# The last store of a row-sum kernel, split by partitions over two issuing engines

## The chip, the cores and the metric

The kernel runs on one core of a Trainium2 chip. The metric is the device time of one execution in microseconds (us); lower is better. Three runs of the kernel before took 160.67, 160.80 and 160.85 us, so its time is their median, 160.8 us.

A core has several engines that run side by side and wait for each other through semaphores. Three matter here: VectorE (DVE in the profile) and ScalarE (ACT) do the arithmetic; SyncE (SP) computes nothing and issues DMAs, the transfers between HBM and the on-chip memory SBUF. ScalarE can issue DMAs too. SBUF has 128 partitions; a transfer of a tile moves one row for each partition.

## The reference

```
batch, seq, dim = 32, 512, 1024
x: (32, 512, 1024) float32, multiplier: 0.5

return (np.sum(x, axis=-1) * multiplier).astype(np.float32)
```

The input has 32 x 512 = 16384 rows of 1024 floats, 64 MB in all. Each row gives one number, so the output is 64 KB.

## The kernel before

Each of the 128 partitions takes 128 rows, in 8 blocks of 16. In the first 7 blocks (112 rows of each partition, `own = 112`) the rows of a partition lie one behind the other in the input; the last block is cut the same way from what is left (`x_last`, `out_last`). So a block is a tile of 128 partitions x 16 rows x 1024 floats, 8 MB, and there are three buffers for blocks (`buf`). The sums of the rows are collected in the tile `res`, 128 partitions x 128 columns, of which the last 16 columns belong to the last block.

SyncE issues all transfers, in the order in which they stand in the code. The loads of the first three blocks are moved ahead of the program's opening barrier (`start_loads_at_entry`); each later load (line 76, the helper `load`) waits until VectorE has done with the block that was in its buffer. The last block comes in five pieces: three into a block's buffer (10 rows, 4 rows, one row and 384 columns of the last), and the rest of the last row into the small tile `end`.

Blocks 0 to 5 are summed on VectorE with one reduction each (line 121) and scaled by the multiplier into `res` (line 127). Of block 6, VectorE sums 8 rows and ScalarE the other 8, one activation per row with an accumulated sum (line 85). Then SyncE issues the early store of the first 112 columns of `res` (line 169). The 16 rows of the last block are shared out: rows 1, 4, 7, 9, 13 and 14 to ScalarE, the others to VectorE (line 95, the helper `dve_sum`). The last row is summed in three cuts by VectorE, and its third sum, `final`, takes the first two in.

The end of the program is what the change touches. `late_act` is the count of the semaphore `act_done` after ScalarE's last row; `done` is the count of `dve_done` after `final`. SyncE waits for `act_done` (line 194), then issues the last store, of the last 16 columns of `res` in all 128 partitions (8 KB, 64 bytes per partition), which itself waits for `dve_done` (line 195). Then it waits until the early store and this one have landed (lines 199 and 200, one instruction in the program). The engines end their programs there, and a closing stretch follows that is not part of the span.

Of the kernel before, what the change touches and what calls it, by code (L numbers as in the profile page):

```python
# [9 lines left out]
def kernel(  # L10
# [13 lines left out]
    nc = tc.nc  # L24
# [4 lines left out]
    P = nc.NUM_PARTITIONS  # L29
# [12 lines left out]
    own = rows - B  # L42
# [3 lines left out]
    out_last = out_flat[P * own : N].rearrange("(p c) -> p c", p=P)  # L46

    def sbuf(name, *shape):
        return ctx.enter_context(nc.sbuf_tensor(name, list(shape), fp32)).ap()
# [4 lines left out]
    res = sbuf("res", P, rows)  # L54
# [4 lines left out]
    def sem(name):  # L59
        return nc.alloc_semaphore(name=name)  # L60

    dve_done = sem("dve_done")
    act_done = sem("act_done")
    counts = {"dve": 0, "act": 0}

    def marks(i, engine):

        s = dve_done if engine == "dve" else act_done
        i.then_inc(s, 1)
        counts[engine] += 1  # L70
        return counts[engine]
# [36 lines left out]
    for b in range(n_blocks - 1):  # L108
# [11 lines left out]
        done = marks(  # L120
            nc.vector.reduce_sum(  # L121
                out=sums[:, c0 : c0 + h], in_=t[:, 0:h, :], axis=mybir.AxisListType.X
            ),
            "dve",
        )
        freed.append(done)
        scaled = nc.vector.tensor_single_scalar(  # L127
            out=res[:, c0 : c0 + h],
            in_=sums[:, c0 : c0 + h],
# [45 lines left out]
    for k, (lo, hi) in enumerate(((0, 10), (10, 14), (14, 15))):  # L175
# [4 lines left out]
        late_act = marks(i, "act") if k == len(landed) - 1 else None  # L180
# [10 lines left out]
    final.wait_op(landed_end[1], 17, "sem-ge")  # L191
    done = marks(final, "dve")

    nc.sync.wait_ge(act_done, late_act)
    store = nc.sync.dma_start(out=out_last, in_=res[:, own:])
    store.wait_op(dve_done, done, "sem-ge")
    stored = sem("stored")
    store.then_inc(stored, 16)
    nc.sync.wait_ge(early_stored, 16)
    nc.sync.wait_ge(stored, 16)  # L200

    def start_loads_at_entry(nc_):

# [60 lines left out]
```

## Time and profile before

| | |
|---|---|
| median of three runs | 160.8 us |
| span of the profiled execution, first to last instruction of the program | 159.3 us |
| loads of x | 67.11 MB, DMA engines busy 98.1% of the span |
| VectorE busy | 119.8 us (75%) |
| ScalarE busy | 16.3 us (10%) |
| last store, issue on SyncE | 157.89 us, 0.34 us long |
| last store, issue to landing | 1.4 us |
| waits at the end (line 200) | 28 ns from 159.3 us |

The profile is of one execution, and its times count from the first instruction of the program. The span is shorter than the device time, which also takes in what the launch puts around the program. A DMA issue is the work of the issuing engine's sequencer alone (SPq is SyncE's, ACTq would be ScalarE's); the packets follow on the 16 DMA engines, and the transfer has landed when its semaphore has reached its count. The issue's length is not the transfer's.

### The profile page before, as it was taken

Reading aid. Unit: us, or ns where it says so; the run is one execution under the profiler, and the core shown is the slowest. Engines: PE = TensorE matmul, PEld = TensorE weight load, DVE = VectorE, ACT = ScalarE, POOL = GpSimd, SP = SyncE. Lnnn points to the kernel's source line nnn. Section 1 sums busy time; section 2 is a strip of 40 time slices with the busy share of each in tenths; the row PEclk is TensorE's granted clock in tenths of the full one; section 3 lists DMA queues with packets and bytes.
Section 4 is the critical chain, followed back from the end, with each engine's and each line's share of the span. In section 5 each row is a group of like instructions: output and inputs, shape, how many; then the busy total and the mean of one; then the engine's idle time right before and its main releaser. Section 6 shows DMA issues by size and latency. Waiting matters only on the chain.

```text
span 159.3 us, 123 instructions
## 1 busy us (share of the span) xinstructions
DVE 119.8 (75%) x38; ACT 16.3 (10%) x29; POOL 0.2 (0%) x4
## 2 busy tenths in 40 slices
DVE  0000059998699968999599995999959999598376
ACT  3000000000000000000000000000000000397384
POOL 0000000000000000000000000000000000000000
DMA  7996996997998969969969969969989799798994
GB/s 263 526 526 263 526 526 263 526 477 313 526 428 362 526 280 510 526 263 526 526 263 526 526 263 526 494 296 526 444 345 526 345 444 526 329 473 350 424 396 151
DMA packets 2016, 67.18 MB, mean 422 GB/s; under 512 B 480, under 2 KB 736, under 8 KB 864
## 3 DMA queue, kind: packets, MB, share of 16 engines
q1 hardware_dynamic: 2016, 67.18, 98.1%
HBM read 67.11 MB, written 0.07 MB: 422 GB/s over the span
## 4 chain that ended last, share of the span: by engine, by line
DMA 74%; DVE 24%; another core or an unknown queue 1%; SPq 0%; issue 0%
DMA xb<-in_x_dram 74%; DVE sums L121 22%; DVE xb L95 1%; DVE end L95 0%; SPq L76 0%; DVE res L127 0%; DVE res L95 0%
## 5 line engine op out<-in xcount | busy, mean ns | idle before, releaser
L121 DVE TENSOR_REDUCE sums<-xb 128x16 f32<-128x16384 f32 (+1 forms) x7 | 112.0, 16001 | 33.3 <-DMA xb<-in_x_dram 33.3
L85 ACT ACTIVATE xb<-xb 128x1024 f32<-128x1024 f32 x14 | 14.6, 1044 | 139.1 <-DMA xb<-in_x_dram 139.1
L95 DVE CUSTOM_DVE_ANT_0 xb<-xb 128x512 f32<-128x512 f32 (+1 forms) x10 | 6.0, 655 | 4.4 <-DMA xb<-in_x_dram 4.4
L85 ACT ACTIVATION_READ_ACCUMULATOR xb<-xb 128x1 f32 x14 | 2.6, 187 | 0.0
L85 ACT ACT_TABLE_LOAD x1 | 1.3, 1283 | 2.4 <-PEq L26 2.4
L127 DVE TENSOR_SCALAR res<-sums 128x16 f32<-128x16 f32 (+1 forms) x7 | 1.2, 174 | 0.2
L95 DVE DVE_READ_ACCUMULATOR2_ANT res<- 128x1 f32 x10 | 0.8, 82 | 0.0
L95 DVE CUSTOM_DVE_ANT_0 end<-end 128x176 f32<-128x176 f32 (+1 forms) x2 | 0.7, 326 | 0.0
L95 DVE DVE_READ_ACCUMULATOR2_ANT end<- 128x1 f32 x2 | 0.2, 82 | 0.0
L245 POOL MEMSET const-bfloat16-1.0<- 128x1 bf16 x1 | 0.1, 101 | 0.0
L245 POOL MEMSET const-uint8-127<- 128x1 uint8 x1 | 0.1, 101 | 0.0
L245 POOL MEMSET const-float32-0.0<- 128x1 f32 x1 | 0.1, 98 | 0.2 <-issue 0.2
L245 POOL MEMSET const-float32-1.0<- 128x1 f32 x1 | 0.1, 98 | 0.0
## 6 DMA issues: line engine op xcount, KB each, us to landing
xb<-in_x_dram SPq DMA_DIRECT2D x1, 5120.0 KB, 33.6
xb<-in_x_dram SPq DMA_DIRECT2D x1, 2048.0 KB, 36.4
xb<-in_x_dram SPq DMA_DIRECT2D x1, 704.0 KB, 20.8
end<-in_x_dram SPq DMA_DIRECT2D x1, 176.0 KB, 19.2
end<-in_x_dram SPq DMA_DIRECT2D x1, 144.0 KB, 10.8
xb<-in_x_dram SPq DMA_DIRECT2D x7, 40.8
out_dram<-res SPq DMA_DIRECT2D x1, 56.0 KB, 10.6
out_dram<-res SPq DMA_DIRECT2D x1, 8.0 KB, 1.4
```

The source lines that it names most:

```text
L85: return nc.scalar.activation(out=t[:, r, :], in_=t[:, r, :], func=mybir.ActivationFunctionType.Copy, scale=mul, accum_out=res[:, col : co ...
L95: return nc.vector.tensor_tensor_reduce(out=row[:, 0:mid], in0=row[:, 0:mid], in1=row[:, mid:], scale=scale, scalar=0.0, op0=ADD, op1=ADD, ...
L121: nc.vector.reduce_sum(out=sums[:, c0 : c0 + h], in_=t[:, 0:h, :], axis=mybir.AxisListType.X),
L127: scaled = nc.vector.tensor_single_scalar(out=res[:, c0 : c0 + h], in_=sums[:, c0 : c0 + h], scalar=mul, op=mybir.AluOpType.mult,)
L245: nc = _bacc.Bacc("TRN2", target_bir_lowering=False, num_devices=1)
```

## The change

The last store becomes two DMAs. The first takes partitions 0 to 63 and is issued by SyncE, the second takes partitions 64 to 127 and is issued by ScalarE. Each engine waits for `act_done` and each DMA for `dve_done`, as the one store did. Each has a semaphore of its own, and SyncE waits for both at the end. In the built program SyncE has as many DMAs as before, its last with 64 rows in place of 128; ScalarE has one DMA, behind its last activation, where it had none; SyncE's last wait is two instructions, for the first half, and for the second half with the early store.

```diff
-    nc.sync.wait_ge(act_done, late_act)
-    store = nc.sync.dma_start(out=out_last, in_=res[:, own:])
-    store.wait_op(dve_done, done, "sem-ge")
-    stored = sem("stored")
-    store.then_inc(stored, 16)
+    stored = []
+    for k, queue in enumerate((nc.sync, nc.scalar)):
+        lo, hi = k * P // 2, (k + 1) * P // 2
+        queue.wait_ge(act_done, late_act)
+        store = queue.dma_start(out=out_last[lo:hi, :], in_=res[lo:hi, own:])
+        store.wait_op(dve_done, done, "sem-ge")
+        stored.append(sem(f"stored{k}"))
+        store.then_inc(stored[k], 16)
     nc.sync.wait_ge(early_stored, 16)
-    nc.sync.wait_ge(stored, 16)
+    for s in stored:
+        nc.sync.wait_ge(s, 16)
```

## The prediction

> **What bounds the kernel now.** I first read the chain of work that ended last, in order of time, for its tail, because the change touches nothing ahead of the last store.
>
> ```profile
> 118.55 36.35 DMA xb<-in_x_dram
> ...
> 157.50 0.31 DVE end L95
> 157.81 0.01 DVE res L95
> ```
>
> The columns are start, length (both us) and what. Up to 154.9 us the chain is input loads and the sums behind them; 2.9 us of last sums follow, and the chain's last engine work, the final sum on VectorE, ends at 157.82. The page names the DMA load as 74% of the span and VectorE as 24%; neither is touched. What is left is 157.82 to the end of the span at 159.35, some 1.5 us that belong to the store alone. The timeline of that stretch shows who is busy in it:
>
> ```profile
> 156.67 1.06 ACT L85 ACTIVATE xb<-xb 128x1024 f32<-128x1024 f32 x1 [0.59 <-DMA xb<-in_x_dram]
> 157.50 0.31 DVE L95 CUSTOM_DVE_ANT_0 end<-end 128x145 f32<-128x145 f32 x1
> 157.63 0.19 ACT L85 ACTIVATION_READ_ACCUMULATOR xb<-xb 128x1 f32 x1
> 157.74 0.08 DVE L95 DVE_READ_ACCUMULATOR2_ANT res<- 128x1 f32 x1
> 157.89 0.34 SPq L195 DMA_DIRECT2D out_dram<-res  x1
> ```
>
> ScalarE's last sum ends at 157.63 + 0.19 = 157.82, the same moment as VectorE's, 157.74 + 0.08 = 157.82. So both of the store's conditions come together, and ScalarE is free at the moment when SyncE issues. The issue runs from 157.89 to 158.23. Next, the DMA engines in a window from 158.3 to 159.3 (40 slices of 25 ns; each digit is the busy share in tenths):
>
> ```profile
> DMA  0000000000000000026755421000000000000000
> ...
> DMA packets 144, 0.01 MB, mean 8 GB/s; under 512 B 144, under 2 KB 144, under 8 KB 144
> ```
>
> All 144 packets of the store lie in slices 17 to 24, so from 158.72 to 158.92. Last, the waits of the DMA queue's own engine and the issues:
>
> ```profile
> SPq L200 <- DMA out_dram<-res: 1.1, 1, 1.1
> ...
> out_dram<-res SPq DMA_DIRECT2D x1, 56.0 KB, 10.6
> out_dram<-res SPq DMA_DIRECT2D x1, 8.0 KB, 1.4
> ```
>
> SyncE's final wait is 1.1 us long and is for this store; the store of the other columns, issued at 147.06, landed 10.6 us later at 157.66 and is out of the way. So the store's 1.46 us, from 157.89 to 159.35, split into 0.34 of issue, 0.49 of silence, 0.20 of packets, 0.37 of silence until it has landed, and 0.05 until SyncE's wait is over. Only 0.20 of it moves data. In the two silences (0.86) no engine and no DMA is busy: they are latency.
>
> **The change, part by part.** The profiled execution's span is 159.35; I put the 1.45 us around it at the median's 160.8, of which the three runs (160.67 to 160.85) stand within 0.1%. Neither start-up nor the stream of loads changes, so the sum is made on the store's 1.46 us.
>
> *SyncE's half.* It keeps its two waits and its issue at 157.89. The twelve load issues in the summary of line 76 take a median of 328 ns whether they carry 8 MB or 144 KB, and the two stores 368 and 344 ns. So an issue does not pay for bytes. All of them have 128 rows, so no row shows whether it pays for rows. From above: nothing saved, 0.34. From below: half, 0.17. I take 0.34, because the rows show it constant over a range of 1 to 1000 in size. Its packets halve (64 rows): 0.20 us becomes something between 0.10 (goes with the packets) and 0.20 (if the stretch is set by the engines starting one after another). I take 0.15. This half lands at 157.89 + 1.41 − 0.05 = 159.25, 0.05 earlier than now.
>
> *ScalarE's half.* New on ScalarE are a wait for its own last sum and a DMA issue that waits for VectorE. Nothing stands behind them on ScalarE, and only SyncE waits for their result. On SyncE the same pair cost 0.07 from the last sum to the issue, and SyncE's is done by 157.89; I give ScalarE the same start. How long a DMA issue takes on ScalarE no row shows, for this kernel never makes one there. Bounds: 0.33 from SyncE's usual row, and 1.28 from the costliest thing that ScalarE's sequencer does here, its table load at the start. Three issues of SyncE lie at the very start, when the queue is used for the first time:
>
> ```profile
> L76 SPq DMA_DIRECT2D xb<-in_x_dram x3: 382/432/435, 0.0 to 0.9; - x3
> ```
>
> They take 382 to 435 ns instead of 328. ScalarE's issue will be a first one too, and stands beside another issue, so I take 0.40, from the nearest row.
>
> *Whether the two issues overlap.* This decides. If they do, ScalarE's half has issued at 157.89 + 0.40 = 158.29, 0.06 behind the old store; with 0.05 less of packets its landing is unchanged, +0.0. If descriptors for the two can only be made one after the other, ScalarE's issue does its work after SyncE's ends at 158.23, and lands 0.34 + 0.06 − 0.05 = 0.35 later. No row has two engines issuing at once, so both ends stay in the range. The nearest row is the three entry issues again: they start at 0.00, 0.43 and 0.91, the second and third 50 ns longer than the first, so an issue with another's descriptors still in progress gets no faster but slower; they share something. That leans me to the serial end.
>
> The Trainium skill states it outright: Perfetto Trace Analysis, section "DMA Instruction — HWDGE (DVE, Sync)", says that the descriptor generator is one block that the sequencers share, locked for exclusive use until all descriptors of a DMA are made, with the wait for the lock counted in the issue. The longer entry issues agree with it but do not prove it. Its DMA: Bandwidth & Descriptors, section "Rules for kernel authors", speaks against this very edit: two transfers to disjoint partition halves serialize on the same DMA engines, so one 128-partition transfer should be used. By the first of these rules the sum is +0.35, by the second, which concerns the packets alone, it is at most the 0.20 us that packets take now, so near 0.
>
> *The last waits.* SyncE now has two wait instructions at the end, one for each half. As long as ScalarE's half lands last, the first is over before the second ends and costs nothing. If SyncE's half came last, the second would follow it, and the pair at line 194 and 195 shows the step: line 194 takes 17 ns and the next instruction begins some 47 ns after it began, so +0.05.
>
> *Sum.* 0.00 (SyncE's half, now hidden behind the other) + 0.34 (waiting for SyncE's issue) + 0.06 (first issue on ScalarE) − 0.05 (fewer packets in each half) = +0.35: 160.8 + 0.35 = 161.15, which I round up to 161.2, since of the two unknown prices in it, ScalarE's issue has far more room above than below. What a measurement of this kernel can tell from no change is about 0.2%, 0.32 us: 160.48 to 161.12 is "same". The forecast is slower, by a hair over that.
>
> **Rivals.**
>
> *A: the issues overlap; no change.* For it: ScalarE is free at 157.82, and of the store's 1.46 us, 0.86 are silences that two transfers can sit through side by side. The DMA engines have room, since even their busiest slice of 25 ns is at seven tenths. Against it: the lengthened entry issues. Time: 160.8 + 0.06 − 0.05 + up to 0.05 of the last wait = 160.8 to 160.9.
>
> *B: the time goes with rows; faster.* Both the issue and the making of descriptors behind it would be row by row, and ScalarE's half runs at the same time. Then the issue halves, 0.34 to 0.17, the first silence halves as well, 0.49 to 0.25, and the packets give 0.05: 160.8 − 0.17 − 0.24 − 0.05 = 160.34. It decides from the point where the savings pass 0.32, so only if both halve. For it: no row has fewer than 128 rows, so nothing refutes it. Against it: the first packets come half a microsecond after the issue ends, and an end that waits on rows would let the first rows' packets out early; the issues' constancy speaks for a cost per DMA. In the Trainium skill, Perfetto Trace Analysis, section "DMA Optimizations", is on this side: balancing DMAs over the engines may help where descriptor generation is the bottleneck. By the rows that is 0.34 of 159.35 us here.
>
> *C: ScalarE's first issue is far slower than SyncE's.* ScalarE has not made a DMA before this point, and a first use on its sequencer, with its code and its queue, can cost what its table load costs: 1.28 instead of 0.34. That gives 160.8 + 0.94 − 0.05 = 161.7 overlapped, 162.0 behind SyncE's issue. For it: on the store's path nothing hides the excess, and the entry issues of SyncE show that first ones are longer. Against it: there the excess is 0.05 to 0.11, not 0.9; and ScalarE's first activation takes 1.06 us in the timeline, hardly more than the page's mean of 1.044.
>
> **How the numbers follow.** Serial issues 0.40, A 0.22, B 0.12, C 0.26. The forecast's own range is 161.0 to 161.4 (lock held for a part of the issue only, to an issue of 0.43 and no gain in packets); about four fifths of it lie above 161.12. So slower: 0.32 + 0.26 and a little of A, where ScalarE's issue takes 0.7 or so, 0.02: 0.60. Same: 0.08 + 0.20 = 0.28. Faster: 0.12. The likeliest time is 161.2. The range from 160.65 to 162.0 takes in all of the forecast and A and some two thirds of C (an issue of up to 1.28 behind SyncE's); it leaves out B and the rest of C, 0.12 + 0.08 = 0.20.
>
> **What would show it.** Serial: ScalarE's DMA issue starts near 157.9 and is 0.65 to 0.75 us long, or starts near 158.2 and is 0.33 to 0.43; packets come in two bursts 0.3 to 0.4 apart, and SyncE's last wait is for ScalarE's half. A: both issues some 0.35 to 0.4 long over the same time, one burst, and a span within 0.1 of 159.35. B: SyncE's issue near 0.17 and its packets before 158.5. C: ScalarE's issue over 0.8 us, or a gap over 0.6 between its end and its packets. The prediction is wrong if the span does not grow by what ScalarE's half is late, or if anything ahead of 157.8 moves.

## The result and the profile after

The changed kernel takes 161.22 us (median of 6 runs, 161.08 to 161.33) against 160.81 (6 runs, 160.63 to 160.94) for the kernel before in the same measurement: a ratio of 1.0029, 95% interval 1.0019 to 1.0039, or 0.3 to 0.6 us slower. The profiled execution's span is 159.87 us.

Everything ahead of the store is as it was: the final sum on VectorE ends at 157.80 (157.82 before). This is the end of the changed kernel's timeline, with the columns as before:

```profile
157.48 0.31 DVE L95 CUSTOM_DVE_ANT_0 end<-end 128x145 f32<-128x145 f32 x1
157.60 0.18 ACT L85 ACTIVATION_READ_ACCUMULATOR xb<-xb 128x1 f32 x1
157.72 0.08 DVE L95 DVE_READ_ACCUMULATOR2_ANT res<- 128x1 f32 x1
157.86 0.54 SPq L198 DMA_DIRECT2D out_dram<-res  x1
157.88 0.54 ACTq L198 DMA_DIRECT2D out_dram<-res  x1
```

The two issues do stand side by side, 0.02 us apart. But each is 0.54 us long, where the one issue before took 0.34, for half of the rows. Next, the DMA engines in a window of 2 us from the first issue's start, 157.86 to 159.86, so that a slice is 50 ns; the lines for the queues say that q1 is SyncE's and q10 is new, ScalarE's:

```profile
DMA  0000000000000000000000012210032200000000
...
DMA packets 160, 0.01 MB, mean 4 GB/s; under 512 B 160, under 2 KB 160, under 8 KB 160
...
q10 hardware_dynamic: 80, 0.00, 2.3%
q1 hardware_dynamic: 80, 0.00, 2.2%
```

And the same window from the issue's start of the kernel before, 157.89 to 159.89:

```profile
DMA  0000000000000000066410000000000000000000
```

Before, the packets come in slices 16 to 20. After, there are two bursts, from slice 23 and from slice 29: by the packet records the first starts 1.17 us after the issue (0.84 before), the second 0.28 later. The waits and the issues say the same:

```profile
SPq L204 <- DMA out_dram<-res: 1.4, 2, 1.2
...
out_dram<-res SPq DMA_DIRECT2D x1, 4.0 KB, 1.7
out_dram<-res ACTq DMA_DIRECT2D x1, 4.0 KB, 2.0
```

SyncE's own half now lands 1.7 us after its issue, not 1.4, and ScalarE's half 2.0 us after its own. SyncE waits twice, 1.4 us in all: 1.2 us for its half, and 0.3 more for ScalarE's (the three figures are rounded).

From here on "the stretch" is the time from the first issue of the last store to the end of the span, in the records of the trace. It was 1.457 us and is 2.014: 0.557 more. Each kernel left one trace, so how far the stretch differs from run to run is not measured; but the changed kernel and `e3` below, whose last stores are the same, have 2.014 and 2.022. The loads and sums ahead of it vary more: over all the traces the final sum ends between 157.74 and 158.21 us. So the stretch tells apart what the medians blur. Each kernel's difference from the kernel before in the medians agrees with that in the stretch to 0.17 us at worst.

### The profile page after: what moved, and what is told of

Read it like the earlier page. It is cut to its first block, busy times and chain, and to the rows that moved or that the text cites. A ratio compares the mean times of both kernels' runs of the same rounds, so it can differ in the third digit from the quotient of the medians.

```text
span 159.9 us, 126 instructions
## 1 busy us (share of the span) xinstructions
DVE 119.9 (75%) x38; ACT 16.3 (10%) x29; POOL 0.2 (0%) x4
## 4 chain that ended last, share of the span: by engine, by line
DMA 74%; DVE 23%; another core or an unknown queue 1%; SPq 0%; issue 0%
DMA xb<-in_x_dram 74%; DVE sums L121 22%; DVE xb L95 1%; DVE end L95 0%; SPq L76 0%; DVE res L127 0%; DVE res L95 0%
```

## The experiments

Twelve kernels were measured against the kernel before and one another. All of them leave the loads and the sums alone.

### Is it ScalarE, the rows, or the two side by side?

The first four tell apart three theories: that the issues stretch each other (contention), that ScalarE's first DMA is slow, and that a DMA of 64 rows is slow for itself.

*The whole store from ScalarE* (`e1`), from the kernel before:

```diff
-    nc.sync.wait_ge(act_done, late_act)
-    store = nc.sync.dma_start(out=out_last, in_=res[:, own:])
+    nc.scalar.wait_ge(act_done, late_act)
+    store = nc.scalar.dma_start(out=out_last, in_=res[:, own:])
```

> The whole last store (128 rows) issued by ScalarE alone, as its first and only DMA; nothing else is changed from the kernel before. Contention theory (the two issues stretch each other because they share what makes descriptors): alone, ScalarE's issue is as short as SyncE's was, 0.33 to 0.40 us, its first packet comes 0.5 us after the issue's end, the span's last stretch from the issue to the end is 1.45 to 1.55 us, and the time is 160.8 to 160.9. First-use theory (ScalarE's first DMA is slow whatever stands beside it): the issue takes 0.5 us or more, the stretch is 1.7 us or more, the time 161.05 or more.

Measured: 160.74 us, ratio 1.0001 (0.9992 to 1.0010). The issue's length comes from the summary of its line; the numbers are ns, shortest, median and longest:

```profile
L195 ACTq DMA_DIRECT2D out_dram<-res x1: 369/369/369, 158.1 to 158.1; - x1
```

The stretch is 1.488. The store as ScalarE's first and only DMA costs 0.03 us more than from SyncE. The first-use theory, the prediction's rival C, has fallen.

*Both halves from SyncE* (`e2`), from the changed kernel:

```diff
-    for k, queue in enumerate((nc.sync, nc.scalar)):
+    for k, queue in enumerate((nc.sync, nc.sync)):
```

> Both halves issued by SyncE, one behind the other; ScalarE issues nothing. Contention theory: each issue takes 0.33 to 0.38 us, since only one is ever at work; the first half's packets start where the old store's did (0.84 us after the issue's start), the second half's 0.35 to 0.45 later, and the time is +0.35 to +0.45, 161.15 to 161.25: as long as the two-engine version, so the second engine buys nothing. Theory that rows are what costs (a DMA of 64 rows has a longer issue, 0.54, for itself): the issues take 0.54 each, and the time is +0.7 or more, 161.5.

Measured: 161.69 us, ratio 1.0061 (1.0046 to 1.0076), stretch 2.387.

```profile
L198 SPq DMA_DIRECT2D out_dram<-res x2: 531/532/533, 158.1 to 158.7; - x2
```

Both issues take 0.53 us though no other engine issues beside them. The contention theory had 0.33 to 0.38 here; 0.54 is what the rows theory said. The second issue starts 0.62 us after the first, and its packets come 1.18 us after its own start, as the first one's do (1.17): one behind the other, the second DMA is not delayed. Against one engine, the second engine saves 2.387 − 2.014 = 0.37 us of waiting for the sequencer. The Trainium skill (DMA: Bandwidth & Descriptors, section "Issuing engines are not separate DMA queues") says that issuing from several engines saves just that, and that it is usually small beside the DMA itself. The trace agrees on the saving; here it is more than half of an issue and a sixth of the stretch.

*ScalarE's half not its first DMA* (`e3`), from the changed kernel:

```diff
-    nc.sync.wait_ge(dve_done, early_dve)
-    early = nc.sync.dma_start(out=out_rows, in_=res[:, 0:own])
+    nc.scalar.wait_ge(dve_done, early_dve)
+    early = nc.scalar.dma_start(out=out_rows, in_=res[:, 0:own])
```

> The changed kernel, with the early store of 112 columns issued by ScalarE too, so that its half of the last store is not its first DMA. Contention theory: nothing changes in the last store, both issues still take 0.5 to 0.56 us, the second burst still comes 0.28 after the first, time as the changed kernel, 161.1 to 161.4. First-use theory: both issues fall back to 0.34 to 0.4, the stretch from issue to end to 1.5 to 1.7 us, time 160.8 to 161.0.

Measured: 161.47 us, ratio 1.0043 (1.0026 to 1.0060). The issues are 0.56 and 0.53 us, the bursts 0.27 apart, the stretch 2.022: no change in the last store, as contention and rows both had it. The time is at the top of the interval of the changed kernel or above: in the profile the final sum ends at 158.12 here, 0.3 later, ahead of the store. Some 0.2 of that is there by 60 us in these traces (the third block's sum starts at 60.67 and not 60.47), long before the early store is issued, so it is not the early store's doing. The other 0.1 arises in the last loads, with which the early store now competes from a queue of its own; that this is the reason was not tested.

*SyncE's half alone* (`e4`), from the changed kernel; the other half is not stored:

```diff
-    for k, queue in enumerate((nc.sync, nc.scalar)):
+    for k, queue in enumerate((nc.sync,)):
```

> SyncE's half alone: the last 16 columns of partitions 64 to 127 are not stored. Contention theory: the issue takes 0.33 to 0.35 us and the stretch from its start to the end of the span is 1.40 to 1.46, time 160.75 to 160.8; rows cost nothing in the issue. Theory that 64 rows have a longer issue for themselves: 0.54 in the issue and 161.0 or more. Theory that an issue is paid by the row (the prediction's rival B): 0.17 in the issue and 160.4.

Measured: 160.99 us, ratio 1.0017 (1.0008 to 1.0027), stretch 1.736.

```profile
L198 SPq DMA_DIRECT2D out_dram<-res x1: 523/523/523, 158.0 to 158.0; - x1
```

Half of the store, alone, is slower than all of it: 0.18 us in the issue, and its packets start 1.165 after the issue and not 0.839. Contention in the issue has fallen, and so has the prediction's rival B. Of the 0.557, 0.279 is here, without a second DMA.

### Is it 64 rows, or fewer than 128?

*Split by columns* (`e5`): 8 columns of all 128 partitions from each engine, from the changed kernel:

```diff
-        lo, hi = k * P // 2, (k + 1) * P // 2
+        lo, hi = k * B // 2, (k + 1) * B // 2
...
-        store = queue.dma_start(out=out_last[lo:hi, :], in_=res[lo:hi, own:])
+        store = queue.dma_start(out=out_last[:, lo:hi], in_=res[:, own + lo : own + hi])
```

> The last store is split by columns: 8 columns of all 128 partitions from SyncE, the other 8 from ScalarE, both behind the last sums. The SyncE half alone of the split by partitions took 0.52 us to issue where 128 rows took 0.34, so the contention theory has fallen for the issue. Form theory (a DMA with 64 rows has a long issue for itself, one with 128 rows does not, whoever stands beside it): both issues take 0.34 to 0.38 us, the first burst of packets starts 0.84 after the issue's start, and only the delay of the second burst is left, 0.28 to 0.4; the stretch from the issue to the end of the span is 1.7 to 1.9 us, time 160.95 to 161.1. If issues side by side did stretch each other, 0.5 or more in each, and the time is 161.2 or more.

Measured: 160.94 us, ratio 1.0014 (1.0005 to 1.0024), stretch 1.622. The issues and, in a window of 2 us from the first issue, the DMA engines:

```profile
L198 SPq DMA_DIRECT2D out_dram<-res x1: 345/345/345, 158.0 to 158.0; - x1
L198 ACTq DMA_DIRECT2D out_dram<-res x1: 370/370/370, 158.0 to 158.0; - x1
```

```profile
DMA  0000000000000000069951000000000000000000
```

Side by side, the two issues are as short as either one alone, and the packets lie in one burst from slice 16 on, the second set 0.05 us behind the first. That was expected to stay at 0.28 or more. The stretch came out shorter than expected for this reason.

*96 rows* and *32 rows* from SyncE alone (`e6`, `e7`), from the kernel before; the other rows of the last 16 columns are not stored:

```diff
-    store = nc.sync.dma_start(out=out_last, in_=res[:, own:])
+    store = nc.sync.dma_start(out=out_last[0:96, :], in_=res[0:96, own:])
```

> One last store from SyncE with 96 rows; the last 16 columns of partitions 96 to 127 are not stored. If every count of rows but 128 takes the long way, the issue is 0.52 us, as with 64 rows, and the stretch to the end 1.73. If the issue gets longer with fewer rows, it lies between 0.34 and 0.52, about 0.43. If only the even halves of 64 are slow, it is 0.34 and the stretch 1.45.

> One last store from SyncE with 32 rows; the last 16 columns of partitions 32 to 127 are not stored. If every count of rows but 128 takes the long way at a fixed price, the issue is 0.52 us and the stretch 1.65 to 1.73. If the issue gets longer with fewer rows, 0.6 us or more. If it were paid by the row on the long way, shorter than with 64 rows: 0.43 or less.

Measured, 96 rows: 160.76 us, ratio 1.0003 (0.9994 to 1.0012), stretch 1.445; 32 rows: 160.61 us, ratio 0.9995 (0.9986 to 1.0004), stretch 1.387. One line from each:

```profile
L195 SPq DMA_DIRECT2D out_dram<-res x1: 358/358/358, 157.9 to 157.9; - x1
```

```profile
L195 SPq DMA_DIRECT2D out_dram<-res x1: 352/352/352, 158.3 to 158.3; - x1
```

Neither is slow. Of the counts tried, 32, 64, 96 and 128, only 64 is, and no theory of "fewer rows cost more" can explain that.

*ScalarE's half alone* (`e8`), partitions 64 to 127, from the kernel before:

```diff
+    nc.scalar.wait_ge(act_done, late_act)
+    store = nc.scalar.dma_start(out=out_last[P // 2 :, :], in_=res[P // 2 :, own:])
```

> ScalarE's half alone: the last 16 columns of partitions 0 to 63 are not stored, and SyncE has no last store. If the second burst is late only because SyncE's DMA is being made beside it, ScalarE's half alone has an issue of 0.54 us, its first packet 1.17 after the issue's start and the stretch 1.74 to 1.78, time 160.95 to 161.05. If ScalarE's half is late for itself (other partitions, another queue), its first packet is at 1.43, the stretch 2.0, and the time 161.2 or more.

Measured: 161.04 us, ratio 1.0021 (1.0011 to 1.0030), stretch 1.757; the first packet comes 1.18 after the issue's start.

```profile
L195 ACTq DMA_DIRECT2D out_dram<-res x1: 523/523/523, 157.8 to 157.8; - x1
```

That is SyncE's half alone to within 0.02 us, so 64 rows cost this on either engine, in the lower half from SyncE and in the upper one from ScalarE. And ScalarE's burst, at 1.43 after its own issue in the changed kernel, is late by 0.25 because of the DMA beside it, not for itself.

### What is different about 64 rows

The instruction lists of the built programs, which the profiles do not show, give a lead. Each DMA carries its shape and, for most, a flag:

```
before      SP   rows 128 x 16   ant_dge_precooked true
changed     SP   rows  64 x 16   (no flag)
changed     ACT  rows  64 x 16   (no flag)
32 rows     SP   rows  32 x 16   ant_dge_precooked true
```

By its name the flag marks a DMA whose shape the library has worked out ahead of time; what the chip does differently without it the profiles do not show. In builds with 16, 32, 48, 65, 80, 96, 112, 120 and 128 rows the last store has the flag; with 64 rows it has not, with 8, 15 or 16 columns and from partition 0, 32 or 64. Why 64 is left out was not found, and a store of 64 rows with the flag was not built. Three kernels test whether the flag is the price.

*128 rows without the flag* (`e9`), from the kernel before:

```diff
     nc.sync.wait_ge(act_done, late_act)
+    nc.dge_precook = False
     store = nc.sync.dma_start(out=out_last, in_=res[:, own:])
```

> Stores of 32, 96 and 128 rows took 0.35 us to issue, a store of 64 rows 0.52. In the built programs every DMA carries a flag for a shape that was worked out ahead of time (ant_dge_precooked), but for those of 64 rows, which the library leaves unflagged. Here the one last store of 128 rows from SyncE is built without the flag, and nothing else is changed from the kernel before. Flag theory (the missing flag is the price, not the rows): issue 0.52 to 0.55 us, first packet 1.17 after the issue's start, the stretch to the end 1.75 to 1.80, time +0.25 to +0.35. Rows theory (64 rows are slow on the chip, with or without the flag): issue 0.34, first packet at 0.84, time unchanged.

Measured: 161.07 us, ratio 1.0023 (1.0014 to 1.0032), stretch 1.804. First the issue, then the window of 2 us from its start:

```profile
L196 SPq DMA_DIRECT2D out_dram<-res x1: 546/546/546, 157.9 to 157.9; - x1
```

```profile
DMA  0000000000000000000000006631000000000000
```

One store of 128 rows from one engine, and without the flag it has the long issue, and its packets begin in slices 23 and 24 like those of 64 rows. The flag's absence costs 1.804 − 1.457 = 0.35 us: 0.20 in the issue and 0.14 between its end and the first packet. (The stretch and the time, 0.36 more, stand at the upper end of what the flag theory gave or just beyond it.) The loads, which stand ahead of the edit in the code, still take 328 ns to issue. So the missing flag is enough for the long issue and the late packets, with 128 rows as with 64; the count of rows makes 0.02 us of difference in the issue (0.546 against 0.523).

*The cut at 96* (`e10`): 96 rows from SyncE, 32 from ScalarE, both flagged, from the changed kernel:

```diff
-        lo, hi = k * P // 2, (k + 1) * P // 2
+        lo, hi = ((0, 96), (96, P))[k]
```

> The change with the cut at partition 96: SyncE stores 96 rows, ScalarE 32, both flagged, all else as in the changed kernel. Flag theory: issues of 0.34 to 0.38 us, first packets at 0.84 and 0.05 later, SyncE's wait ends 0.15 to 0.17 after that of one store, as with the split by columns: stretch 1.58 to 1.62, time +0.13 to +0.20. If a split by partitions costs for itself, it stays near the changed kernel: stretch 1.9 to 2.0, time +0.4.

Measured: 160.94 us, ratio 1.0012 (1.0003 to 1.0021), stretch 1.617. The issues, and the window of 2 us from the first one:

```profile
L198 SPq DMA_DIRECT2D out_dram<-res x1: 358/358/358, 158.0 to 158.0; - x1
L198 ACTq DMA_DIRECT2D out_dram<-res x1: 406/406/406, 158.1 to 158.1; - x1
```

```profile
DMA  0000000000000000045520000000000000000000
```

The same change with the cut elsewhere costs 0.16 us in the stretch and not 0.56. ScalarE's issue, 0.41, and the time, 0.23 more in the medians, are each 0.03 above what was expected.

*The split by columns without the flag* (`e12`), `nc.dge_precook = False` ahead of both stores of `e5`:

> The split by columns (8 of all 128 partitions from SyncE, 8 from ScalarE) with both DMAs built without the flag. Flag theory: issues of 0.53 us, the first burst of packets at 1.17 and the second some 0.28 later, as in the changed kernel, so stretch 2.0 and time +0.45 to +0.6. If the second burst's delay belongs to 64 rows, it comes 0.05 later as with the flag: stretch 1.9. If making descriptors without the flag is paid by the row, the delay is 0.5 and the stretch 2.25.

Measured: 161.31 us, ratio 1.0037 (1.0024 to 1.0049), stretch 2.075. The issues and its window of 2 us:

```profile
L199 SPq DMA_DIRECT2D out_dram<-res x1: 546/546/546, 157.9 to 157.9; - x1
L199 ACTq DMA_DIRECT2D out_dram<-res x1: 551/551/551, 157.9 to 157.9; - x1
```

```profile
DMA  0000000000000000000000005420045410000000
```

Two bursts again, 0.27 us apart, with 128 rows. So the delay of the second burst goes with the missing flag too, not with 64 rows, and is not paid by the row. (Each DMA is 4 KB here as in the changed kernel, so whether it is paid by the byte was not tested.)

### What is left of the price with the flag

In `e5` and `e10` the packets of the two DMAs overlap, and yet the stretch is 0.16 us longer. The trace's semaphore records (us after the first issue) show where:

```
              landing counts of the first DMA    of the second
before        1.247 to 1.413 (16)
e5, columns   1.243 to 1.409 (16)                1.424 to 1.578 (16)
e10, 96/32    1.236 to 1.403 (16)                1.413 to 1.574 (16)
```

The semaphore of each of these DMAs rises by 16 counts, and 16 of its packets are of 4 bytes, one for each count. The counts come mostly about 10 ns apart, and those of the second DMA begin only when the first one's are over, though its packets were 0.05 to 0.07 us behind. In `e5` the last count is 0.165 later than before, as much as the stretch is longer, while the last packet of data ends only 0.045 later (1.087 against 1.042). If the counts are the price, fewer of them must cut it.

*The cut at 120* (`e13`), from `e10`:

```diff
-        lo, hi = ((0, 96), (96, P))[k]
+        lo, hi = ((0, 120), (120, P))[k]
```

> The split by partitions with the cut at 120: SyncE stores 120 rows, ScalarE 8, both flagged. With the flag the two bursts of packets came 0.05 to 0.07 us apart, but the 16 landing increments of the second DMA began only when the 16 of the first were over, about 10 ns each, and that is what was left of the split's price (stretch 1.62 against 1.46). Increment theory: a count of rows that 16 does not divide is spread over fewer DMA engines, so 120 rows give 15 increments and 8 rows 8, and the stretch shrinks to 1.52 to 1.57, time +0.05 to +0.12. Theory that a second DMA costs 0.16 for itself (its issue, its wait): stretch 1.60 to 1.65, time +0.15 to +0.20.

Measured: 160.88 us, ratio 1.0009 (1.0000 to 1.0018), stretch 1.565.

```profile
q1 hardware_dynamic: 135, 0.01, 4.3%
q10 hardware_dynamic: 16, 0.00, 0.4%
...
L198 SPq DMA_DIRECT2D out_dram<-res x1: 422/422/422, 157.8 to 157.8; - x1
L198 ACTq DMA_DIRECT2D out_dram<-res x1: 578/578/578, 157.9 to 157.9; - x1
```

135 packets are 120 rows and 15 counts, 16 are 8 rows and 8 counts. The stretch is in the range of the increment theory; the time, 0.14 more in the medians, lies between the two theories. It is no clean proof: the issues grew, to 0.42 and 0.58 us, and the order turned round. The 8 counts of ScalarE's DMA come first, at 1.165 to 1.227, and SyncE's 15 behind them, at 1.322 to 1.462. So SyncE's own half landed last, and the wait for ScalarE's half was still to come: from the last count to the end of the span it is 0.10 us here, and 0.04 in the kernel before and in `e5` and `e10`. Of the 0.108 by which the stretch is longer, 0.049 is thus in the landing and 0.06 in the second wait. In all three splits with the flag the counts of the two DMAs do not overlap; that this is all of the 0.16 in `e5` and `e10` is likely, not shown.

No version that stores everything beat the kernel before. The nearest, the store moved whole to ScalarE, is level with it.

## Why the prediction was right, and where it was not

*The time* came out at 161.22 where 161.2 was forecast, but the forecast sum was +0.35 and the stretch grew by 0.557; in medians, 0.41 with an interval of 0.31 to 0.63. In the timed runs, device time and span differ by 1.3 us throughout (161.2 and 159.9, for one), so the profiled execution before, which the prediction put at the median, took about 159.35 + 1.33 = 160.68: it was a quick one. That does not enter the sum, which starts from the median. As the next points show, one term was 0.28 too low and others a little too high. That leaves the sum 0.2 us short of the stretch, but the medians, whose interval takes in both, came out only 0.06 above the sum, and rounding 161.15 up met most of that. The hit on the digit is partly luck. Of the forecast's signs two came: two bursts of packets, 0.28 apart where 0.3 to 0.4 was said, and a last wait for ScalarE's half. The two in the issue, 0.65 to 0.75 us long or a start near 158.2, did not.

*What bounds the kernel*: right. Loads and sums did not move, and the whole change lies behind 157.8.

*SyncE's half*, put at 0.00 and "hidden behind the other": this step failed. The prediction took 0.34 for the issue "because the rows show it constant over a range of 1 to 1000 in size", while it said that all rows had 128 rows, and bounded it from above at "nothing saved". The unknown lay on the other side: the issue took 0.54 and the silence behind it 0.63, not 0.49. Alone, this half makes the stretch 0.28 longer (`e4`), and a missing flag is enough to do that (`e9`).

*"They share something", and the issues one after the other*, +0.34: half right. Two issues do not exclude each other: 0.536 and 0.539 side by side, 0.523 each alone (`e4`, `e8`). What comes one after the other shows behind the issue: without the flag the second set of packets is 0.28 behind the first, with it 0.05 to 0.07. So the term was 0.28, not 0.34, at another place. That the making of descriptors (the orders for the DMA engines) is what takes turns fits this, but no row shows it. The Trainium skill (Perfetto Trace Analysis, section "DMA Instruction — HWDGE (DVE, Sync)") puts the wait for the shared generator inside the issue's profiled length. Here no 64-row issue was longer beside another one than alone by more than 0.04 us (0.557 in `e3` against 0.523), so the measurement goes against the place it gives. The three longer issues at the start, on which the leaning rested, are poor evidence for it: in `e2` an issue right behind another one took 0.533 us and the first 0.531, no longer for its neighbour. What made those three longer was not tested.

*ScalarE's first issue*, +0.06: the whole store from ScalarE cost 0.03 more (`e1`). Whether that is the first use is not shown: in `e3`, where its half was not its first DMA, the issue was no shorter. Rival C is out.

*Fewer packets*, −0.05: about 0.02; from the start of the first packet to that of the last it is 0.177 us for SyncE's half and 0.199 for the whole store.

*The last waits*: right. The wait for SyncE's half ends 0.28 before the end and costs nothing. In `e13`, where SyncE's half landed last, the second wait cost the 0.06 for which the prediction had 0.05.

*Rival A*, that the issues overlap and nothing is lost: they overlap, and with the flag (`e5`, `e10`) the loss is still 0.16, of which the working knew nothing: the second DMA's landing counts come late. The Trainium skill's advice against two transfers to partition halves (DMA: Bandwidth & Descriptors, section "Rules for kernel authors") holds: no split gained. Its reason, that the transfers share the DMA engines, is not what cost in the changed kernel, where the packets of the two halves lie apart; where the flag is set they overlap. Whether the sharing makes the landing counts wait for each other no run here shows.

*Rival B*, that time goes by rows: out, by issues of 0.35, 0.36 and 0.34 us with 32, 96 and 128 rows.

The sum as measured, in the stretch: 0.279 for a DMA of 64 rows, which has no flag, against one of 128 rows with it, and 0.278 for the second one's packets behind the first's make the 0.557.

## What to carry to other kernels

A store at the end of a kernel is latency, not bytes: of 1.46 us, 0.2 moved data, and splitting it cut none of that latency and added to it. When a DMA's shape changes, look at what the build makes of it before explaining its time by rows or engines: one count of rows had no flag, and that store of half the size took 0.28 us longer than the whole one; taking the flag from the whole store cost it 0.35. A row that was constant over every size in a trace says nothing about the dimension that never varied in it.

## What the runs showed of the hardware that was not expected

An issue of the last store without the flag took 0.52 to 0.56 us, and its packets started 1.17 to 1.19 us after its start where no other issue stood beside it (`e2`, `e4`, `e8`, `e9`); with the flag, 0.34 to 0.37 and 0.84 to 0.87 (before, `e1`, `e6`, `e7`). Two unflagged DMAs issued together put their packets 0.27 to 0.28 us apart (the changed kernel, `e3`, `e12`), two flagged ones 0.05 to 0.07 (`e5`, `e10`). The later packets were ScalarE's each time, in `e3` too, where its issue had started 5 ns ahead of SyncE's. Where two flagged DMAs ended together, their landing counts came one DMA after the other, some 10 ns each, so that the second was seen to have landed 0.17 us after the first, with 128 rows (`e5`) as with 32 (`e10`).
